# Loading the first half of x first, sharing one bank between the first two products of eight pairs, and moving the second layer's memory keys in a two-layer fp32 network

## The chip, the cores and the metric

The kernel runs on one core of one Trainium2 chip. The metric is device time in microseconds (us) of one execution; with several executions, their median. TensorE (PE in the profile) multiplies into banks of PSUM, VectorE (DVE) and ScalarE (ACT) read those banks and work on SBUF, GpSimd (POOL) works on SBUF, and SyncE (SP) issues the transfers (DMA).

## What is computed

Two layers over 1024 tokens of width 1024, with a memory of 256 rows, all in fp32:

```python
def reference(x, mem, norm_g, final_g, mem_norm_g, ...):
    mem_n = rmsnorm(mem, mem_norm_g)
    h = x
    for i in range(DEPTH):                 # 2
        j = i // 2
        if i % 2 == 0:
            h = even_layer(h, mem_n, ...)
        else:
            h = odd_layer(h, mem_n, ...)
    return rmsnorm(h, final_g)

def even_layer(h, mem_n, g, w_in, pool_w, pool_scale, w_mem_kv, w_out):
    u = rmsnorm(h, g)
    za, rq, rk, rv, xq, gate = split_cols(u @ w_in, EVEN_SPLITS)
    y = concat([pool_mixer(za), retention(rq, rk, rv), mem_attention(xq, mem_n, w_mem_kv)]) * silu(gate)
    return h + y @ w_out

def odd_layer(h, mem_n, ...):
    u = rmsnorm(h, g)
    q, kc, vc, ks, vs, kw, vw, gl, xq, gate = split_cols(u @ w_in, ODD_SPLITS)
    y = concat([nsa_attention(q, kc, vc, ks, vs, kw, vw, gl), mem_attention(xq, mem_n, w_mem_kv)]) * silu(gate)
    return h + y @ w_out
```

`mem_attention` needs keys and values of the memory, `mem_n @ w_mem_kv`, in both layers. `nsa_attention` compresses keys (`kc`, `vc`), selects blocks by them, and attends to the selected blocks (`ks`, `vs`) and to a window (`kw`, `vw`).

## The kernel before

Activations lie transposed: 128 features on the partitions, 512 tokens (half of the 1024, `HT`) in the free dimension, so one half of x is 8 tiles of 128x512. The fp32 products are made of three matmuls each: `split` (L70, L71) cuts a tile into a rounded high part, cast by ScalarE, and the rest, subtracted by VectorE or by GpSimd, and `mm3` (L77 to L79) multiplies high by high, low by high and high by low. In the names, `wh` and `wl` are the parts of a weight tile, `wr` is the raw one, `uh` and `ul` those of the normalised input. A scheduler fixes the order of each engine's instructions from the program's order; tiles come from pools with a fixed number of buffers, and a tile that takes a buffer waits for the last readers of the one before it.

**Start.** `mem_kv("ev")` (L296) loads the memory (`memT`, two transfers), forms its scaled parts `mu`, its sum of squares `macc`, and multiplies by four weight tiles for the keys (256 columns a matmul) and four for the values (512 columns). Only then `make_u` (L436) loads the first half of x (`x`, four buffers), sums the squares into `acc`, and takes the reciprocal root: the sum over partitions is a matmul with ones (L135), the root's power is taken by GpSimd (L142), VectorE multiplies the identity by it (`dg`, L150), a matmul with ones spreads it over all partitions (L155), ScalarE copies it to `rb` (L158). Then x is loaded a second time, VectorE multiplies each tile by gain and `rb` (`uf`), and it is split. The projections (`ps_mm<-uh,wh`) of the first half follow: pooling, retention, memory attention, gates, two output projections (`out_proj`).

**Half boundary.** The loop over `hf` calls `make_u` for the second half after the first half's last output projection.

**Layer change.** `u_half` (L174) normalises the tiles of the new layer's input, `u_sums` (L182) forms differences of them: the second layer's projections are computed in pairs of weight column blocks by a Strassen scheme over both token halves. Its operands are B11, B21, B22 and T1 to T4, each four tiles of 128x512 in two parts. `strassen` (L226) makes 7 products of 12 matmuls (128x512) for a pair. Two of them need only the first half: B11 and B21. `early` (L206) computes these two ahead for six pairs (kc, vc, q0, q2, q4, q6; `ahead`, L792), while VectorE is still busy with the second half's u; for such a pair `strassen` then makes the other 5. The first product goes to bank a, the second to bank c; ScalarE copies the first out with the scale (L213, tile `p`), VectorE adds the second to it (L220, `sc`). `mem_kv("od")` stands behind them and keeps the memory's parts in the buffers of T4, which is split only afterwards (`u_last`).

**Then** the remaining pairs run, with `rel_tables`, `compress`, `select` (the choice of blocks, L955 on, its scores at L992) and the memory heads between them.

**Start of attention.** `kv_prep` (L1110) fetches the keys and values of each of two groups, four tiles of keys (`kraw`) and four of values (`vraw`) a group, through two buffers called uf, splits the keys, and transposes the values on TensorE (L120). Group 0 is prepared before the first head, group 1 behind the first head's scores.

Of the kernel before, what the change touches and what calls it, by code (L numbers as in the profile page):

```python
# [9 lines left out]
F32 = mybir.dt.float32  # L10
# [9 lines left out]
HT = 512  # L20
# [19 lines left out]
def net(tc, a, out, dbg=None):  # L40
# [128 lines left out]
        return {nm: [[uo.tile([128, HT], F32R, name=f"{nm}{k}{s}", tag=f"{nm}{k}{s}") for s in "hl"] for k in range(4)]  # L169
                for nm in names}  # L170

    def u_late(uo):
        return [[uo.tile([128, HT], F32R, name=f"T4{k}{s}", tag=f"T4{k}{s}") for s in "hl"] for k in range(4)]

    def u_half(U, x, gi, f, rr, rb):
        rb = spread(rr, HT, r=rb)
        for k in range(8):
# [4 lines left out]
    def u_sums(U, x):  # L182
        for k in range(4):
            b11, b12, b22 = x[0][k], x[1][k], x[1][k + 4]
            dve.tensor_tensor(b11, b12, b11, OP.subtract)
            dve.tensor_tensor(b12, b22, b12, OP.subtract)
            dve.tensor_tensor(b22, b22, b11, OP.subtract)
            split(*U["T2"][k], b22)
            dve.tensor_tensor(x[0][k + 4], x[0][k + 4], b22, OP.subtract)
        for nm, f in (("T3", 1), ("T1", 0)):  # L190
            for k in range(4):
                split(*U[nm][k], x[f][k])

    def u_last(U, uo, x):
        U["T4"] = u_late(uo)
        for k in range(4):
            split(*U["T4"][k], x[0][k + 4])

    def product(o, w, x, start):
        for k in range(4):  # L200
# [5 lines left out]
    def early(U, sa, sink, hold, out_t, scale=1.0):  # L206


        ra = wraw(sa)
        pa = bank("a")  # L210
        product(pa, whl(ra[:, :HT], pool), U["B11"], True)
        t = hold()
        act.activation(t, pa, AF.Copy, scale=scale)  # L213
        pc = bank("c")
        product(pc, whl(ra[:, HT:], pool), U["B21"], True)
        d = dr.tile([128, HT], F32, name=f"p1d{len(kept)}")
        kept.append(d)
        sp.dma_start(d, t)
        c = out_t()
        dve.scalar_tensor_tensor(c, pc, scale, t, OP.mult, OP.add)  # L220
        sink(0, 0, c, None)
        return d

# [72 lines left out]
    def mem_kv(pre, acc, slots, mrb):  # L296


        u = []
        first = not memst  # L300
        for k in range(8):
            if k % 4 == 0:
                r = wraw(a["memT"][k:k + 4].rearrange("k p m -> p k m"))
            x = r[:, (k % 4) * NMEM:(k % 4 + 1) * NMEM]
            s = slots[k // 2][k % 2]
            uh, ul = s[:, :NMEM], s[:, NMEM:]
            act.activation(uh, x, AF.Copy, scale=gains[:, 3, k:k + 1])
            dve.scalar_tensor_tensor(ul, x, gains[:, 3, k:k + 1], uh.bitcast(F32), OP.mult, OP.subtract)
            if first:
                add_square(acc, x, NMEM, k == 0)  # L310
            u.append((uh, ul))
        kd = [dr.tile([128, NMEM], F32, name=f"{pre}mkd{h}") for h in range(4)]
        vd = [dr.tile([128, HT], F32, name=f"{pre}mvd{m}") for m in range(2)]
        mkv[pre] = kd, vd
        for h in range(4):
            w = wload(a[pre + "_mk"][h])
            o = bank("s")
            gemm(o[:, :NMEM], w, u)
            if first and h == 0:
                sp.dma_start(ident, a["ident"])  # L320
                memst["rr"] = rstd_of(acc, NMEM, "m")
            if h == 0:
                rb = spread(memst["rr"], NMEM, r=mrb)
            t = tmp.tile([128, HT], F32, name="mkx", tag="uf", bufs=2)
            dve.tensor_tensor(t[:, :NMEM], o[:, :NMEM], rb, OP.mult)
            sp.dma_start(kd[h], t[:, :NMEM])
        yield
        o2 = [bank("s"), bank("s")]
        for c in range(4):
            w = wload(a[pre + "_mv"][c])  # L330
            for kk in range(2):
                k = 2 * c + kk
                for m in range(2):
                    mm3(o2[m], u[k][0][:, m * 128:(m + 1) * 128], u[k][1][:, m * 128:(m + 1) * 128],
                        w[kk][0], w[kk][1], k == 0, k == 7)
        for m in range(2):
            t = tmp.tile([128, HT], F32, name="mvx", tag="uf", bufs=2)
            act.activation(t, o2[m], AF.Copy, scale=memst["rr"][:, m:m + 1])
            sp.dma_start(vd[m], t)
        yield  # L340
# [92 lines left out]
    evx = ExitStack()  # L433
    tm2 = evx.enter_context(tc.tile_pool(name="tm2", bufs=1, reuse_waits="tile"))

    def make_u(srcs, n, gi, pool_, tag, rr=None):  # L436
        def load(k):
            x = up.tile([128, n], F32, name="x", tag="x", bufs=4)
            sp.dma_start(x, srcs[k])
# [7 lines left out]
        rb = spread(rr, n, r=tm2.tile([128, n], F32, name="rb", tag="rb"))  # L447
        u = []
        for k in range(8):
            uf = tmp.tile([128, n], F32, name="uf", tag="uf", bufs=2)  # L450
            dve.scalar_tensor_tensor(uf, load(k), gains[:, gi, k:k + 1], rb, OP.mult, OP.mult)
            uh = pool_.tile([128, n], F32R, name="uh", tag=tag, bufs=16)
            ul = pool_.tile([128, n], F32R, name="ul", tag=tag, bufs=16)
            split(uh, ul, uf)
            u.append((uh, ul))
# [65 lines left out]
    def drain(g):  # L521
        for _ in g:
            pass

    with tc.tile_pool(name="mk0", bufs=1, reuse_waits="tile") as mp_:
        macc, mrb = (mp_.tile([128, NMEM], F32, name=nm) for nm in ("macc", "mrb"))
        slots = [[mp_.tile([128, HT], F32R, name=f"mu{k}{x}") for x in "hl"] for k in range(4)]
        drain(mem_kv("ev", macc, slots, mrb))

    rh = []  # L530
    ep = evx.enter_context(tc.tile_pool(name="ep", bufs=1, reuse_waits="tile"))
    if True:
# [9 lines left out]
        R = [None] * 4  # L542

        for hf in range(2):
            u = make_u([a["xT"][k][:, hf * HT:(hf + 1) * HT] for k in range(8)], HT, 0, up, "u")
            if hf == 0:
                hacc = []
                retm = econst("retm", (128, 4, 128))
# [99 lines left out]
            with tc.tile_pool(name="rp", bufs=1, reuse_waits="tile") as rp:  # L648
# [101 lines left out]
                ret_out(0, n0)  # L750
                ret_out(1, n1)
            if hf == 0:
                out_proj(1, EV_ORDER[1], False)


# [17 lines left out]
    kvs = ctx.enter_context(tc.tile_pool(name="kvs", bufs=1, reuse_waits="tile"))  # L773
    ulx = ExitStack()
    uo = ulx.enter_context(tc.tile_pool(name="uo1", bufs=1, reuse_waits="tile"))
    U.update(u_pool(uo, ("T3", "T1", "T2", "B22")))

    qd = dram2("qd", 12)
    zo = {nm: dram2("o" + nm, n)
# [19 lines left out]
    ahead(("kc", 0), ("vc", 0))  # L799
    u_half(U, X, 1, 1, rh[1], wtile("rb"))  # L800
    u_sums(U, X)
    ahead(("q", 0), ("q", 2), ("q", 4), ("q", 6))
    drain(mem_kv("od", None, u_late(uo), wtile("mrb")[:, :NMEM]))
    u_last(U, uo, X)
    xpx.close()

    def mem_heads(p_, pre, xq, gate, dst, bufs=1, pbufs=1):
# [250 lines left out]
    proj_pair("vc", 0)  # L1058
    proj_pair("q", 0)
    rel_tables()  # L1060
    proj_pair("q", 2)
    compress()
    proj_pair("q", 4)
# [43 lines left out]
        dve.memset(t[:, 0:256], 0.0)  # L1107
        tabs.append(t)

    def kv_prep(g):  # L1110
        for f in range(2):
            c = slice(f * HT, (f + 1) * HT)
            for br in ("s", "w"):
                k = fetch(tmp, zo["k" + br][g][f], "uf", 2, "kraw")
                split(KT[br, g][0][:, c], KT[br, g][1][:, c], k)
                v = fetch(tmp, zo["v" + br][g][f], "uf", 2, "vraw")
                b = bank("t", (128, 4, 128))
                for n in range(4):
                    transpose(b[:, n], v[:, n * 128:(n + 1) * 128])
                split(VN[br, g][0][:, 4 * f:4 * f + 4], VN[br, g][1][:, 4 * f:4 * f + 4], b)  # L1120

    with ExitStack() as oc:
# [147 lines left out]
                proj.pop(0)  # L1270

        proj_step()
        kv_prep(0)
        res = []
        for _ in scores(*units[0], res):
            proj_step()
        kv_prep(1)
        for n, (hf, h) in enumerate(units):
            now, res = res, []
            sg = scores(*units[n + 1], res) if n + 1 < len(units) else iter(())  # L1280
# [149 lines left out]
```

## Time and profile before

| | us |
|---|---|
| median of 3 runs | 2050.36 (2049.96 to 2052.46) |
| the profiled execution | 2047.62 |
| its span in the trace | 2045.8 |
| mean granted clock of TensorE | 0.976 |
| TensorE busy | 1944.2 (95%) |
| VectorE busy | 1276.0 (62%) |
| ScalarE busy | 943.0 (46%) |
| GpSimd busy | 598.7 (29%) |

The span runs from the first to the last instruction of the core; the execution's own time lies 1.8 us above it. Busy time of TensorE includes the overlap of successive matmuls, so a share of 95% doesn't say how fast it works. A row of the waits names the engine and instruction that waited, and what ended the wait. A row of the timeline has start and duration, and in brackets how long the engine had been idle before and what released it.

### The profile page before, as it was taken

The page shows a single profiled execution, that of the slowest core. Times are in us where ns is not written, and L with a number is a line of the kernel's source. Part 1 is how long each engine was busy: PE and PEld are TensorE (multiplying, and loading weights), DVE is VectorE, ACT ScalarE, POOL GpSimd, SP SyncE. Part 2 cuts the span into 40 slices and gives each one's busy share as a digit, 9 for nine tenths or more (in the row PEclk, how much of TensorE's full clock was granted, in tenths as well). Part 3 has the DMA queues.
Part 4 walks back from the last instruction along what each step waited for, and adds up shares of the span by engine and source line. Part 5 has one row for each costly group of instructions (what it writes and reads, how often), then busy time and mean ns, then how long its engine had stood idle before and what let it go on. Part 6 is the DMA issues. An engine that isn't in the chain of part 4 may idle for free.

```text
span 2045.8 us, 28686 instructions
## 1 busy us (share of the span) xinstructions
PE 1944.2 (95%) x9814; PEld 1618.4 (79%) x9814; DVE 1276.0 (62%) x2741; ACT 943.0 (46%) x1867; POOL 598.7 (29%) x615
## 2 busy tenths in 40 slices
PE   5799999999999999799999999998899999999996
PEld 4688888878888877678878788886788888888885
DVE  4667455566645564745439855765666677877675
ACT  4445322334432243431222344544656676767674
POOL 0111110010311002245426643333343444333422
PEclk9899999989999999899999999998899999999998
DMA  6423234442222444476535433337454532151312
GB/s 208 154 82 129 89 107 134 146 141 83 92 93 84 143 152 153 153 209 204 183 114 185 149 106 125 134 108 249 141 177 148 165 99 73 46 172 47 114 37 93
DMA packets 128246, 267.07 MB, mean 131 GB/s; under 512 B 15543, under 2 KB 32707, under 8 KB 128067
## 3 DMA queue, kind: packets, MB, share of 16 engines
q1 hardware_dynamic: 128100, 265.24, 40.0%
q8 instruction: 77, 1.26, 0.3%
q14 instruction: 69, 0.57, 0.1%
HBM read 206.97 MB, written 60.57 MB: 131 GB/s over the span
## 4 chain that ended last, share of the span: by engine, by line
PE 48%; DVE 3%; DMA 2%; issue 1%; ACT 1%; POOL 0%; SPq 0%; DVEq 0%; POOLq 0%; ACTq 0%
PE ps_t L120 5%; PE ps_a L77 3%; PE ps_a L78 3%; PE ps_a L79 3%; PE ps_s L77 3%; PE ps_mm L77 3%; PE ps_mm L79 3%; PE ps_s L78 3%; PE ps_s L79 3%; PE ps_mm L78 3%; PE ps_o L84 2%; PE ps_o L83 2%; PE ps_o L82 2%; PE ps_b L77 2%; PE ps_b L78 2%; PE ps_b L79 2%
## 5 line engine op out<-in xcount | busy, mean ns | idle before, releaser
L70 ACT CAST wh<-wr 128x512 fp32r<-128x512 f32 (+1 forms) x395 | 242.1, 618 | 475.0 <-PE ps_mm L78 312.1
L71 DVE TENSOR_TENSOR wl<-wr,wh 128x512 fp32r<-128x512 f32 (+1 forms) x281 | 213.8, 766 | 173.6 <-ACT wh L70 167.7
L77 PE MATMUL ps_mm<-uh,wh 128*128 128x512 f32 x640 | 253.6, 398 | 2.7 <-ACT uh L70 2.7
L71 POOL TENSOR_TENSOR wl<-wr,wh 128x512 fp32r<-128x512 f32 x114 | 158.6, 1393 | 325.4 <-ACT wh L70 292.2
L79 PE MATMUL ps_mm<-uh,wl 128*128 128x512 f32 x640 | 253.3, 396 | 0.0
L78 PE MATMUL ps_mm<-ul,wh 128*128 128x512 f32 x640 | 253.2, 396 | 0.0
L77 PE MATMUL ps_mm<-yh,wh 128*128 128x512 f32 x512 | 205.9, 408 | 7.0 <-ACT yh L70 4.1
L79 PE MATMUL ps_mm<-yh,wl 128*128 128x512 f32 x512 | 206.6, 405 | 1.8 <-DVE wl L71 1.5
L78 PE MATMUL ps_mm<-yl,wh 128*128 128x512 f32 x512 | 206.9, 404 | 0.0
L71 DVE TENSOR_TENSOR apl<-ps_t,aph 128x512 fp32r<-128x512 f32 x204 | 136.1, 671 | 44.9 <-ACT aph L70 34.2
L70 ACT CAST aph<-ps_t 128x512 fp32r<-128x512 f32 x204 | 114.9, 568 | 87.2 <-PE ps_o L83 45.3
L77 PEld LDWEIGHTS ps_mm<-uh,wh 128*128 128x128 f32 x640 | 121.3, 190 | 28.3 <-ACT uh L70 4.4
L1205 POOL TENSOR_TENSOR Pw<-Pw,arc 128x640 f32<-128x640 f32 (+2 forms) x96 | 96.2, 1002 | 161.2 <-DVE arc L1201 98.2
L78 PEld LDWEIGHTS ps_mm<-ul,wh 128*128 128x128 f32 x640 | 121.4, 190 | 24.6 <-DVE ul L71 0.4
L79 PEld LDWEIGHTS ps_mm<-uh,wl 128*128 128x128 f32 x640 | 121.3, 190 | 24.7
L77 PEld LDWEIGHTS ps_mm<-yh,wh 128*128 128x128 f32 x512 | 96.9, 191 | 29.2 <-ACT yh L70 5.0
L70 ACT CAST wh<-ws 128x512 fp32r<-128x512 f32 x88 | 54.1, 618 | 141.4 <-PE ps_a L78 67.5
L79 PEld LDWEIGHTS ps_mm<-yh,wl 128*128 128x128 f32 x512 | 97.5, 191 | 23.3 <-DVE wl L71 2.6
L78 PEld LDWEIGHTS ps_mm<-yl,wh 128*128 128x128 f32 x512 | 97.5, 190 | 20.4 <-DVE yl L71 0.7
L71 DVE TENSOR_TENSOR wl<-ws,wh 128x512 fp32r<-128x512 f32 x88 | 68.2, 776 | 59.1 <-ACT wh L70 55.7
L1197 ACT ACTIVATE Ps<-Ps,anm 128x512 f32<-128x512 f32 (+3 forms) x96 | 74.6, 777 | 28.3 <-DVE anm L1194 27.9
L1207 ACT ACTIVATE Ps<-Ps,arc 128x512 f32<-128x512 f32 (+3 forms) x96 | 74.7, 778 | 20.7 <-DVE arc L1201 19.5
(893 smaller groups left out, 4820.1 us busy)
## 6 DMA issues: line engine op xcount, KB each, us to landing
wr<-in_ev_gate SPq DMA_DIRECT2D x32, 512.0 KB, 3.5
wr<-in_ev_out SPq DMA_DIRECT2D x32, 512.0 KB, 3.5
wr<-in_od_out SPq DMA_DIRECT2D x64, 256.0 KB, 3.2
oa<-oho SPq DMA_DIRECT2D x52, 256.0 KB, 2.1
oxr<-oa SPq DMA_DIRECT2D x52, 256.0 KB, 2.8
x<-in_xT SPq DMA_DIRECT2D x32, 256.0 KB, 3.6
wr<-in_od_q SPq DMA_DIRECT2D x16, 512.0 KB, 3.7
w<-in_cmp_w SPq DMA_DIRECT2D x16, 512.0 KB, 4.7
```

The source lines that it names most:

```text
L70: act.copy(hi, src)
L71: (eng or dve).tensor_tensor(lo, src, hi.bitcast(F32), OP.subtract)
L77: pe.matmul(o, wh, xh, start=start, stop=False, skip_group_check=skip)
L78: pe.matmul(o, wh, xl, start=False, stop=False, skip_group_check=skip)
L79: pe.matmul(o, wl, xh, start=False, stop=stop, skip_group_check=skip)
L82: pe.matmul(o, wh, xh, start=start, stop=False)
L83: pe.matmul(o, wl, xh, start=False, stop=False)
L84: pe.matmul(o, wh, xl, start=False, stop=stop)
L120: pe.transpose(o, x, ident[:k, :k])
L1197: act.activation(pt, pt, AF.Exp, bias=nm[:, bi:bi + 1], accum_out=su[:, bi:bi + 1])
L1205: pool.tensor_tensor(pt, pt, rc[:, bi:bi + 1].to_broadcast(list(pt.shape)), OP.mult)
L1207: act.activation(pt, pt, AF.Copy, scale=rc[:, bi:bi + 1])
```

## The change

1. **Start.** The identity and the first half's 8 tiles (`xs`) are loaded before the memory and stay in SBUF; the squares go into `xacc`. `make_u` of the first half is called before the memory's products are drained, and multiplies in place in `xs`: these tiles are not loaded again. The second half's `make_u` is called ahead of the first half's last output projection.
2. **Early pairs.** Both products of a pair add up in one bank, taken in turn from a, a, b, c. ScalarE copies it out after the first product (L205) and again after the second (L211). The low parts of both weights are made by VectorE. Two more pairs, xq0 and xq2, are computed ahead: eight.
3. **Memory of the second layer.** `mem_kv("od")` is called behind `rel_tables`, with buffers of its own; T4 is an operand like the others.
4. **Staging.** `kv_prep` takes a function: group 0 is fetched through the six buffers `Pw`, group 1 through the eight `Ps` (two of each of four), all of the attention's pool.

```diff
     def early(...):
         ra = wraw(sa)
-        pa = bank("a")
-        product(pa, whl(ra[:, :HT], pool), U["B11"], True)
+        b = bank("aabc"[len(kept) % 4])
+        product(b, whl(ra[:, :HT]), U["B11"], True)
         t = hold()
-        act.activation(t, pa, AF.Copy, scale=scale)
-        pc = bank("c")
-        product(pc, whl(ra[:, HT:], pool), U["B21"], True)
+        act.activation(t, b, AF.Copy, scale=scale)
         d = dr.tile([128, HT], F32, name=f"p1d{len(kept)}")
         kept.append(d)
         sp.dma_start(d, t)
+        product(b, whl(ra[:, HT:]), U["B21"], False)
         c = out_t()
-        dve.scalar_tensor_tensor(c, pc, scale, t, OP.mult, OP.add)
+        act.activation(c, b, AF.Copy, scale=scale)
         sink(0, 0, c, None)
...
-    def make_u(srcs, n, gi, pool_, tag, rr=None):
+    def make_u(srcs, n, gi, pool_, tag, rr=None, xs=None):
...
-            uf = tmp.tile([128, n], F32, name="uf", tag="uf", bufs=2)
-            dve.scalar_tensor_tensor(uf, load(k), gains[:, gi, k:k + 1], rb, OP.mult, OP.mult)
+            uf = xs[k] if xs else tmp.tile([128, n], F32, name="uf", tag="uf", bufs=2)
+            dve.scalar_tensor_tensor(uf, xs[k] if xs else load(k), gains[:, gi, k:k + 1], rb, OP.mult, OP.mult)
...
+    sp.dma_start(ident, a["ident"])
     with tc.tile_pool(name="mk0", bufs=1, reuse_waits="tile") as mp_:
+        xs = [mp_.tile([128, HT], F32, name=f"xs{k}") for k in range(8)]
+        acc = mp_.tile([128, HT], F32, name="xacc")
+        for k in range(8):
+            sp.dma_start(xs[k], a["xT"][k][:, :HT])
+            add_square(acc, xs[k], HT, k == 0)
...
-        drain(mem_kv("ev", macc, slots, mrb))
+        mem = mem_kv("ev", macc, slots, mrb)
+        u = make_u(None, HT, 0, up, "u", rstd_of(acc, HT), xs)
+        drain(mem)
...
         for hf in range(2):
-            u = make_u([a["xT"][k][:, hf * HT:(hf + 1) * HT] for k in range(8)], HT, 0, up, "u")
...
             if hf == 0:
+                u = make_u([a["xT"][k][:, HT:] for k in range(8)], HT, 0, up, "u")
                 out_proj(1, EV_ORDER[1], False)
...
-    ahead(("q", 0), ("q", 2), ("q", 4), ("q", 6))
-    drain(mem_kv("od", None, u_late(uo), wtile("mrb")[:, :NMEM]))
-    u_last(U, uo, X)
+    ahead(("q", 0), ("q", 2), ("q", 4), ("q", 6), ("xq", 0), ("xq", 2))
...
     rel_tables()
+    with tc.tile_pool(name="mk1", bufs=1, reuse_waits="tile") as mp_:
+        mrb = mp_.tile([128, NMEM], F32, name="mrb1")
+        slots = [[mp_.tile([128, HT], F32R, name=f"mv{k}{x}") for x in "hl"] for k in range(4)]
+        drain(mem_kv("od", None, slots, mrb))
     proj_pair("q", 2)
...
-                k = fetch(tmp, zo["k" + br][g][f], "uf", 2, "kraw")
+                k = stage(zo["k" + br][g][f], "kraw")
...
-        kv_prep(0)
+        kv_prep(0, lambda src, nm: fetch(at, src, "Pw", PW, nm))
...
-        kv_prep(1)
+        turn = iter(range(8))
+        kv_prep(1, lambda src, nm: fetch(at, src, f"Ps{next(turn) % 4}", PB, nm))
```

How instructions stand now: SyncE at the start of the program, before (`x` are the first half's tiles, `ev_mk` the memory's key weights):

```order
L112 DMA c_gains<-in_gains 128x32
L89 DMA wr<-in_memT 128x4x256 x2
L320 DMA c_ident<-in_ident 128x128
L439 DMA x<-in_xT 128x512 x4
L89 DMA wr<-in_ev_mk 128x1024
L439 DMA x<-in_xT 128x512
L89 DMA wr<-in_ev_mk 128x1024 x3
L89 DMA wr<-in_ev_mv 128x1024
```

and after (`xs` are the first half's tiles, `x` now the second half's):

```order
L515 DMA c_ident<-in_ident 128x128
L520 DMA xs_129<-in_xT 128x512
L520 DMA xs_130<-in_xT 128x512
L520 DMA xs_131<-in_xT 128x512
L520 DMA xs_132<-in_xT 128x512
L520 DMA xs_133<-in_xT 128x512
L520 DMA xs_134<-in_xT 128x512
L520 DMA xs_135<-in_xT 128x512
L520 DMA xs_136<-in_xT 128x512
L89 DMA wr<-in_memT 128x4x256 x2
L429 DMA x<-in_xT 128x512 x5
L89 DMA wr<-in_ev_mk 128x1024 x4
```

The memory moved behind eight tiles of x, and its first weights behind five more, of the second half.

VectorE at the start, before, from the memory's sum of squares on (`wl` are low parts of weights, `mkx` finished keys):

```order
L129 TENSOR_TENSOR macc<-macc,sq 128x256 x5
L71 TENSOR_TENSOR wl<-wr,wh 128x512 x2
L140 TENSOR_SCALAR rs<-ps_t 128x2
L150 TENSOR_SCALAR dg<-c_ident,rrkm 128x128 x2
L71 TENSOR_TENSOR wl<-wr,wh 128x512 x4
L325 TENSOR_TENSOR mkx<-ps_s,mrb 128x256
```

and after:

```order
L441 SCALAR_TENSOR_TENSOR xs_129<-xs_129,c_gains,rb 128x512
L441 SCALAR_TENSOR_TENSOR xs_130<-xs_130,c_gains,rb 128x512
L441 SCALAR_TENSOR_TENSOR xs_131<-xs_131,c_gains,rb 128x512
L441 SCALAR_TENSOR_TENSOR xs_132<-xs_132,c_gains,rb 128x512
L441 SCALAR_TENSOR_TENSOR xs_133<-xs_133,c_gains,rb 128x512
L441 SCALAR_TENSOR_TENSOR xs_134<-xs_134,c_gains,rb 128x512
L441 SCALAR_TENSOR_TENSOR xs_135<-xs_135,c_gains,rb 128x512
L441 SCALAR_TENSOR_TENSOR xs_136<-xs_136,c_gains,rb 128x512
L129 TENSOR_TENSOR macc<-macc,sq 128x256
L71 TENSOR_TENSOR ul<-xs_129,uh 128x512
L71 TENSOR_TENSOR ul<-xs_130,uh 128x512
L71 TENSOR_TENSOR wl<-wr,wh 128x512 x2
```

The first weights' low parts now stand behind the eight products of x by `rb` and two low parts of u.

TensorE at the layer change, before, where the first product of kc (B11, bank a) ends and the second (B21, bank c) begins:

```order
L78 MATMUL ps_a_7065<-B113l_6554,wh_7066 128x512
L79 MATMUL ps_a_7065<-B113h_6553,wl_7067 128x512
L77 MATMUL ps_c_7084<-B210h_6555,wh_7085 128x512
L78 MATMUL ps_c_7084<-B210l_6556,wh_7085 128x512
L79 MATMUL ps_c_7084<-B210h_6555,wl_7086 128x512
```

and after, the fifth pair, q4, at the same step:

```order
L78 MATMUL ps_a_7290<-B113l_6530,wh_7291 128x512
L79 MATMUL ps_a_7290<-B113h_6529,wl_7292 128x512
L77 MATMUL ps_a_7290<-B210h_6531,wh_7311 128x512
L78 MATMUL ps_a_7290<-B210l_6532,wh_7311 128x512
L79 MATMUL ps_a_7290<-B210h_6531,wl_7312 128x512
```

Here both products stand one behind the other in one bank. In the pairs before it seven products in all stand between (the order begins with the first products of kc and vc, the spread of the second half's root at L155, ten matmuls of q0's first product, then the second products of kc and vc); in q6 two matmuls do.

At the half boundary the sum of squares (L135, `acc`) stood behind the last matmul of the first half and the spread (L155) directly behind it; now the sum stands behind the first matmul of the last output projection, and 31 matmuls of that projection lie between it and the spread.

More of the change, by code (lines that the diff above doesn't have):

```diff
@@ L170, in u_pool @@
                 for nm in names}
-    def u_late(uo):
-        return [[uo.tile([128, HT], F32R, name=f"T4{k}{s}", tag=f"T4{k}{s}") for s in "hl"] for k in range(4)]
     def u_half(U, x, gi, f, rr, rb):
@@ L189, in u_sums @@
             dve.tensor_tensor(x[0][k + 4], x[0][k + 4], b22, OP.subtract)
-        for nm, f in (("T3", 1), ("T1", 0)):
+        for nm, f, k0 in (("T3", 1, 0), ("T1", 0, 0), ("T4", 0, 4)):
             for k in range(4):
[L192 to L197, printed above, removed]
+                split(*U[nm][k], x[f][k + k0])
     def product(o, w, x, start):
@@ L319, in mem_kv @@
             if first and h == 0:
-                sp.dma_start(ident, a["ident"])
                 memst["rr"] = rstd_of(acc, NMEM, "m")
@@ L775, in net @@
     uo = ulx.enter_context(tc.tile_pool(name="uo1", bufs=1, reuse_waits="tile"))
-    U.update(u_pool(uo, ("T3", "T1", "T2", "B22")))
+    U.update(u_pool(uo, ("T3", "T1", "T2", "B22", "T4")))
     qd = dram2("qd", 12)
@@ L1108, in net, with kv_prep @@
         tabs.append(t)
-    def kv_prep(g):
+    def kv_prep(g, stage):
         for f in range(2):
@@ L1113, in kv_prep @@
             for br in ("s", "w"):
-                k = fetch(tmp, zo["k" + br][g][f], "uf", 2, "kraw")
+                k = stage(zo["k" + br][g][f], "kraw")
                 split(KT[br, g][0][:, c], KT[br, g][1][:, c], k)
-                v = fetch(tmp, zo["v" + br][g][f], "uf", 2, "vraw")
+                v = stage(zo["v" + br][g][f], "vraw")
                 b = bank("t", (128, 4, 128))
```

## The prediction

> **What bounds the kernel now.** First the page: of its 40 slices of 51 us, here TensorE and its granted clock.
>
> ```profile
> PE   5799999999999999799999999998899999999996
> PEclk9899999989999999899999999998899999999998
> ```
>
> TensorE is full except in the first two slices, near slice 16 (the layer change), slices 27 and 28 (the start of attention) and the last. Work taken off other engines is worth nothing elsewhere; what counts is TensorE's waits and the slow clock behind them. So next the waits of TensorE, in order of cost (us in total, times, longest):
>
> ```profile
> PE ps_t L135 <- DVE acc L129: 15.7, 1, 15.7
> PE ps_t L135 <- DVE macc L129: 13.8, 1, 13.8
> PE ps_t L120 <- DMA vraw<-ovs: 7.4, 2, 6.3
> PE ps_t L155 <- DVE dg L150: 6.8, 3, 2.8
> PE ps_t L120 <- DMA vraw<-ovw: 6.2, 2, 3.2
> PE ps_c L77 <- DVE sc L220: 6.0, 1, 6.0
> PE ps_s L79 <- DVE wl L71: 2.9, 1, 2.9
> ```
>
> The first two are the start; the dg wait of 2.8 us is the half boundary; ps_c and ps_s are the layer change; vraw is the start of attention. Then each of these stages by windows (length, busy time of TensorE, weight loads, VectorE, ScalarE, GpSimd, granted clock, DMA share, GB/s):
>
> ```profile
> 0.00:66.40 66.40, 31.39 (x160) 25.73 (x161) 31.91 (x68) 29.09 (x57) 2.12 (x10) 0.85 0.62 204
> 66.40:71.00 4.60, 4.60 (x11) 3.62 (x12) 4.58 (x7) 1.85 (x3) 0.00 (x0) 0.53 0.64 203
> 427.40:439.40 12.00, 8.64 (x23) 6.39 (x23) 8.74 (x18) 4.00 (x7) 2.43 (x2) 0.57 0.53 173
> 806.40:883.90 77.50, 63.21 (x295) 51.96 (x294) 51.92 (x87) 33.10 (x62) 19.92 (x11) 0.91 0.48 154
> 883.90:890.00 6.10, 6.10 (x14) 4.28 (x14) 5.29 (x6) 2.29 (x4) 3.78 (x3) 0.50 0.43 138
> 1049.80:1136.30 86.50, 84.60 (x458) 72.46 (x456) 68.00 (x118) 26.65 (x47) 57.26 (x57) 0.98 0.51 168
> 1397.00:1441.00 44.00, 34.77 (x158) 28.30 (x158) 25.90 (x69) 25.96 (x58) 20.69 (x24) 0.88 0.96 317
> 1441.00:1453.30 12.30, 6.89 (x31) 5.67 (x32) 4.81 (x9) 4.94 (x9) 3.00 (x3) 0.58 0.53 166
> ```
>
> The clock is a second cost: behind each stage with waits lies a stretch near 0.5. The timeline shows what that does to one 128x512 matmul (start, duration):
>
> ```profile
> 67.42 0.63 PE L78 MATMUL ps_mm<-ul,wh 128*128 128x512 f32 x1
> 67.85 0.63 PE L79 MATMUL ps_mm<-uh,wl 128*128 128x512 f32 x1
> 71.74 0.39 PE L78 MATMUL ps_mm<-ul,wh 128*128 128x512 f32 x1
> 71.97 0.39 PE L79 MATMUL ps_mm<-uh,wl 128*128 128x512 f32 x1
> ```
>
> They follow each other in 0.43 us at half clock and in 0.23 at full, so half of the busy time at half clock is lost. Every TensorE price below goes by starts (0.23), not by durations.
>
> **The change part by part.** *Start.* The timeline:
>
> ```profile
> 1.18 0.97 SPq L89 DMA_DIRECT2D wr<-in_memT  x2
> 10.91 0.33 SPq L89 DMA_DIRECT2D wr<-in_ev_mk  x1
> 14.39 1.14 ACT L70 CAST wh<-wr 128x512 fp32r<-128x512 f32 x2 [1.24 <-DMA wr<-in_ev_mk]
> 15.06 0.58 PE L77 MATMUL ps_s<-mu0h,wh 128*128 128x256 f32 x1 [0.23 <-ACT wh L70]
> 57.29 0.69 DVE L129 TENSOR_TENSOR acc<-acc,sq 128x512 f32<-128x512 f32 x1 [0.63 <-ACT sq L128]
> 58.12 1.84 PE L135 MATMUL ps_t<-ones,acc 128*128 128x1 f32 x8 [15.66 <-DVE acc L129]
> 64.33 0.58 ACT L158 COPY rb<-ps_t 128x512 f32<-128x512 f32 x1 [5.13 <-PE ps_t L155]
> 64.95 1.41 DVE L451 SCALAR_TENSOR_TENSOR uf<-x,c_gains,rb 128x512 f32<-128x512 f32 x2 [2.78 <-ACT rb L158]
> 66.40 1.22 PE L77 MATMUL ps_mm<-uh,wh 128*128 128x512 f32 x2 [2.11 <-ACT uh L70]
> ```
>
> Before: memory products 15.1 to 42.5 (58.12 less 15.66), 27.4 us; then nothing until the sum of squares; the projections run from 66.4, the first 4.6 us at 0.53, so in effect from 68.6. After: eight tiles of 256 KB are 2.1 MB, at the 317 GB/s of the attention window 6.6 us, landed about 9; eight adds of squares at 0.69 behind them end about 12. From the sum to rb took 58.1 to 64.9, 6.8 us: rb about 19. Eight uf at 0.7 end about 25. The first weights of the memory are now issued behind all that SyncE has queued and wait for a buffer that the memory's squares free late, about 18.5; landing took 3.5, so 22. Their low halves stand on VectorE behind the eight uf and two ul: the products start about 27. Then 27.4 us of products, with waits of 1 to 5 us (second weights; dg of the memory now behind two wl): they end at 55 to 59.5, and the projections follow at once at full clock. I take 59.5, since VectorE also has eight ul to make among them: gain 68.6 - 59.5 = **9**. Bounds: 14 with no wait and a start 1 us earlier, 2 where the products start at 34.
>
> *Half boundary.*
>
> ```profile
> 430.20 2.05 PE L155 MATMUL ps_t<-dg,ones 128*128 128x512 f32 x2 [2.75 <-DVE dg L150]
> 434.36 1.22 PE L77 MATMUL ps_mm<-uh,wh 128*128 128x512 f32 x2 [0.61 <-ACT uh L70]
> ```
>
> The second half's loads and squares now begin during the first half, and some 30 matmuls (7 us) stand between the sum's row and the spread's, as long as the 6.8 us chain. Gone: 2.75 + 0.61, and half of what ran at half clock, the 2.05 of the spread and the 5.0 of projections from 434.4 to 439.4: 3.5. I leave 0.4 for the cover being tight: **6.5**, bounds 4 and 7.
>
> The Trainium skill, "TensorE: Matmul & The Clock Gate", Part 1 (the clock gate), has the clock fall after about 3.4 us of idle. The row speaks against it: a wait of 2.75 us and a clock of 0.57. By the page the slow stretch isn't this wait's, and this part would give 2.75 + 0.61 less the 0.4, 3.0.
>
> *Layer change.* Timeline rows, then groups of 806 to 884:
>
> ```profile
> 816.42 5.50 DVE L178 SCALAR_TENSOR_TENSOR x<-x,c_gains,rb 128x512 f32<-128x512 f32 x8 [3.44 <-ACT rb L158]
> 836.19 0.59 ACT L213 ACTIVATE p<-ps_a 128x512 f32<-128x512 f32 x1
> 839.51 0.80 PE L77 MATMUL ps_c<-B210h,wh 128*128 128x512 f32 x1 [5.98 <-DVE sc L220]
> ```
>
> ```profile
> L71 DVE TENSOR_TENSOR wl<-wr,wh 128x512 fp32r<-128x512 f32 x16 | 10.7, 687 | 6.9 <-ACT wh L70 6.8
> L220 DVE SCALAR_TENSOR_TENSOR sc<-ps_c,p 128x512 f32<-128x512 f32 x6 | 4.1, 685 | 8.6 <-PE ps_c L79 8.6
> L71 POOL TENSOR_TENSOR wl<-wr,wh 128x512 fp32r<-128x512 f32 x7 | 15.3, 2200 | 14.0 <-ACT wh L70 14.0
> ```
>
> TensorE's work in the window: six pairs of 24 matmuls and 48 of the memory's at 0.23 (44.2), 96 of 256 columns at half (11.0, an estimate from the 0.23), sums and spreads 1.8: 57 of 77.5. Lost: 20.5, and half of the 6.1 behind it, 3.05: 23.5. After: eight pairs, 192 x 0.23 = 44.2, against the u chain on VectorE. Its sc are gone (4.1), the memory's steps too; 16 wl come, 12 of them inside the chain (12 x 0.69 = 8.2). The spread stands after two products, so rb comes about 813.6 instead of 816.4, and by its rows at 0.6 to 0.7 the chain ends about 848, while the pairs end about 853 and cover it. Where both products of a pair share a bank, the second waits for the copy. In TensorE's order other products lie between, but at two of the eight only two matmuls or none: 0.8 each. The second bound is the 5.98 above, which came from an eviction queued behind u steps; ScalarE's queue has casts of the u chain ahead of its copies too, so it is kept for a rival. With 1.9 of waits here, and 1.6 for the memory's products in their new place among pairs (theirs waited 2.9 for wl here): **20**, bounds 14 and 23.
>
> The Trainium skill, "PSUM — Partial Sum Buffer", summary of rules, has a matmul write another bank while one is read. If nothing lay between, all eight pairs would pay the 0.59 copy and its hand-over, 6 to 8 us in all, and the sum would be 35.
>
> *Select.* In 1049.8 to 1136.3 VectorE is busy 68.0 of 86.5, making the selection beside pairs on TensorE. Two pairs of xq give up two products each, 48 x 0.23 = 11 us, and most of that lay here: the stage shrinks towards 75.5 with VectorE's 68.0, a chain of dependent steps, still to do. Of these 11 I take back **-2**, bounds 0 and -4.
>
> *Attention.*
>
> ```profile
> 1441.62 0.63 PE L120 MATMUL ps_t<-c_ident,vraw 128*128 128x128 f32 x4 [3.01 <-DMA vraw<-ovw]
> 1449.31 1.09 PE L120 MATMUL ps_t<-c_ident,vraw 128*128 128x128 f32 x4 [3.18 <-DMA vraw<-ovw]
> ```
>
> The second group's tiles come one by one through two buffers. In 1441 to 1453.3 TensorE idles 5.4, with 2.4 of the 3.01 ahead of the window 7.8, and loses 2.9 of 6.89 to the clock: 10.7. With eight buffers I leave 1.7, and 0.5 for loads that crowd the first group (the DMA share there is 0.96): **8.5**, bounds 4 and 11. The 6.3 for the first vraw stays: its load hangs on the last projections.
>
> Sum: 9 + 6.5 + 20 - 2 + 8.5 = 42. The profiled execution took 2047.62 (span 2045.8), so 2005.6; it lies 2.7 under the median of 2050.36, so **2008**.
>
> **The rivals.** *The shared bank stalls the pairs* (slower): each second product waits until ScalarE, behind a cast that waits for VectorE, has copied the first. At 5.98 a pair this costs 48, the gain is gone and the time is 2056; it decides from 5.2 a pair. For it: the same wait at 839.51, and the copies among casts. Against: seven products between in most places. 0.04.
>
> *The start gains nothing.* VectorE works on uf and ul first, the memory's weights come late, products end at 66 to 68: 2017. For it: the weights stand behind 17 transfers. 0.13.
>
> *The moved work stalls where it goes.* The memory's weights pass through two buffers among pairs that need their own, and select waits on VectorE: its ten transfers of 3.5 us take 35 us against 23 of products, 12 back, 2020. For it: VectorE's 68.0 in select and the DMA share of 0.51 there. Against: the pairs around it have work to put between. 0.13.
>
> *The clock's loss stays.* If the slow stretches don't hang on the removed waits, 2.3 + 3.5 + 3.05 + 2.9 don't come back: 2020. The rows speak against it, since each stretch follows a wait. It is what the rule of the Trainium skill's clock page, above, would make of waits under 3.4 us. 0.07.
>
> *All covers hold*: start and attention reach their upper bounds, 7.5 more: 2000. 0.08.
>
> **How the numbers follow.** Forecast 0.55; its own range is 2000 to 2016, as the five parts won't all lie at the same bound. With the rivals at 2017 to 2020 and a stall or two beside them, 1994 to 2026 leaves out the slower rival and thin tails. This kernel's times spread by 0.1%, so 0.2% (4 us) is what can be told from no change: faster 0.94, same 0.02, slower 0.04.
>
> **What would show it.** Right: the first memory product at 26 to 28, no wait of several us between it and the second half; no dg wait and a clock of 1 at the half boundary; pairs without gaps for 46 to 48 us behind the last sum, a Strassen product directly behind; no vraw wait above 2 for the second group. Wrong: a wait of ps_a, ps_b or ps_c on ScalarE's p1 of over 1 us in several pairs; waits on wr of the memory's weights among the pairs; slow-clock stretches where no wait stands ahead.

## The result, and the profile after

The changed kernel takes 2018.80 us (median of 4 runs, 2017.64 to 2021.65) against 2050.85 (median of 4 as well): a ratio of 0.9845, 95% interval [0.9828, 0.9862], 32 us. The profiled execution took 2021.65, the longest of the four, with a span of 2019.8 where before had 2045.8; a second profile of the same program, taken later beside experiments, has a span of 2013.3. Both are used below, since what differs between them can't be the change; whether both ran on the same chip isn't known.

The page of the first, slices counted from 0: the first slice has 4 for TensorE, the second is full, and the dips of before at slices 16 and 28 are gone. One at slice 27 is left, and single ones at 17 and 22 are new: there lie the memory's new place and select.

```profile
PE   4999999999999999989999899998999999999996
PEclk9999999999999999999999999998999999999998
```

The starts of the same instructions in three traces (timeline, us) show where the time went:

| | before | after | after, second profile |
|---|---|---|---|
| first projection of the first half | 66.4 | 63.1 | 62.5 |
| last sum of squares before the layer change | 805.5 | 791.6 | 791.0 |
| first Strassen product with T2 | 883.9 | 844.7 | 842.4 |
| last product before the attention | 1394.5 | 1378.0 | 1372.2 |
| end | 2045.8 | 2019.8 | 2013.3 |

By the second profile: 14.5 us are gained up to the layer change (forecast: 15.5), 7.8 between there and the attention (forecast: 18), 10.2 from there on (forecast: 8.5). The sum is 32.5, where 42 was forecast.

TensorE's waits now (us in total, times, longest):

```profile
PE ps_t L135 <- DVE xacc L129: 13.7, 1, 13.7
PE ps_mm L77 <- ACT yh L70: 10.4, 2, 9.0
PE ps_t L155 <- DVE dg L150: 8.1, 3, 5.0
PE ps_b L77 <- ACT mv3l L298: 4.2, 1, 4.2
PE ps_s L77 <- ACT wh L70: 3.8, 1, 3.8
PE ps_s L79 <- DVE wl L71: 3.7, 1, 3.7
PE ps_b L77 <- DVE sc L245: 3.6, 1, 3.6
PE ps_a L77 <- ACT wh L70: 2.2, 1, 2.2
PE ps_a L77 <- ACT p L205: 1.0, 2, 0.7
```

The two waits for sums of squares that cost 15.7 and 13.8 have become one of 13.7, the wait of 6.0 for VectorE's sum at the layer change is gone, and so are those for vraw; of the last, the part at the first values now stands at yh (9.0, start of attention). New are the first wh and wl (ps_s, the start) and mv3l (the memory's new place); sc at L245 (select, L254 before) grew from 1.3 to 3.6. p at L205 is the copy between the two products of one bank: 1.0 in all.

Windows of the start and of the half boundary (length, TensorE, weight loads, VectorE, ScalarE, GpSimd, clock, DMA share, GB/s), then the start's waits and VectorE's queue there:

```profile
23.00:64.00 41.00, 30.30 (x154) 26.30 (x155) 24.50 (x47) 15.89 (x32) 1.08 (x1) 0.92 0.44 140
416.00:430.00 14.00, 14.00 (x66) 11.52 (x64) 6.05 (x9) 4.86 (x8) 0.60 (x1) 1.00 0.51 170
```

```profile
24.10 0.58 PE L77 MATMUL ps_s<-mu0h,wh 128*128 128x256 f32 x1 [3.75 <-ACT wh L70]
28.59 0.58 PE L79 MATMUL ps_s<-mu0h,wl 128*128 128x256 f32 x1 [3.69 <-DVE wl L71]
42.29 1.22 PE L155 MATMUL ps_t<-dg,ones 128*128 128x256 f32 x2 [4.98 <-DVE dg L150]
44.44 0.58 PE L77 MATMUL ps_s<-mu0h,wh 128*128 128x256 f32 x1 [0.92 <-DVE mkx L315]
```

```profile
21.00 5.39 DVE L441 SCALAR_TENSOR_TENSOR xs<-xs,c_gains,rb 128x512 f32<-128x512 f32 x8 [0.63 <-ACT rb L158]
26.64 1.29 DVE L71 TENSOR_TENSOR ul<-xs,uh 128x512 fp32r<-128x512 f32 x2
27.84 1.29 DVE L71 TENSOR_TENSOR wl<-wr,wh 128x512 fp32r<-128x512 f32 x2
39.20 1.29 DVE L71 TENSOR_TENSOR wl<-wr,wh 128x512 fp32r<-128x512 f32 x2 [4.24 <-ACT wh L70]
41.76 0.48 DVE L150 TENSOR_SCALAR dg<-c_ident,rrkm 128x128 f32<-128x128 f32 x2
```

The half boundary is as forecast: no idle, clock 1.00. At the start two memory products run at 24.1, but then TensorE stands 3.7 us until VectorE, through with the eight uf and two ul, has made the first wl (27.84): the first product with a low part, for which the forecast had 27, comes at 28.6. Later it waits 5.0 for dg. The memory's squares were long summed (the last ended at 35.0, the sum over partitions ran at 36.8); ahead of dg on VectorE stand four wl, and the first two wait 4.24 us for their casts (39.20), as ScalarE itself waits 4.4 us for that weight tile. Its transfer comes late: SyncE needs from 19.9 to 35.0 to issue the four tiles of key weights.

The memory's new place among the Strassen pairs, with ScalarE and VectorE ahead of the stall:

```profile
888.12 0.51 ACT L298 ACTIVATE mv2h<-wr,c_gains 128x256 fp32r<-128x256 f32 x1 [5.56 <-DMA wr<-in_memT]
888.66 0.48 DVE L299 SCALAR_TENSOR_TENSOR mv2h<-wr,c_gains,mv2h 128x256 fp32r<-128x256 f32 x1 [3.77 <-ACT mv2h L298]
889.06 0.68 DVE L245 TENSOR_TENSOR sc<-ps_b,u 128x512 f32<-128x512 f32 x1
889.89 0.47 PE L77 MATMUL ps_b<-T10h,wh 128*128 128x512 f32 x1 [4.17 <-ACT mv3l L298]
```

ScalarE stood 5.6 us at the memory's second transfer. VectorE's step of the memory (mv2h) waits for ScalarE, and behind it stands the sum `sc<-ps_b,u` of the pair before, which reads bank b; the next product into bank b starts 0.15 us after that sum ends (889.74), 4.2 us late. The row names mv3l because it ended last, at 889.82, but this product reads nothing of the memory; in a run below (memory transfers ahead) the same wait is put down to the sum, again 0.15 us after its end. In the second profile the two waits around the memory measure 3.6 (mv3l) and 3.6 (q2's pair behind it, whose weights were issued only at 910.2, behind the memory's eight weight tiles), with a slow-clock stretch of 3.4 us after each.

### The profile page after: what moved, and what is told of

Same layout as the page of the kernel before. It is cut to its first block, busy times and chain, and to the rows that moved or that the text cites. A ratio compares the mean times of both kernels' runs of the same rounds, so it can differ in the third digit from the quotient of the medians.

```text
span 2019.8 us, 28659 instructions
## 1 busy us (share of the span) xinstructions
PE 1937.2 (96%) x9814; PEld 1611.9 (80%) x9814; DVE 1276.8 (63%) x2753; ACT 942.8 (47%) x1869; POOL 570.2 (28%) x601
## 4 chain that ended last, share of the span: by engine, by line
PE 85%; DVE 7%; DMA 3%; ACT 2%; issue 2%; POOL 1%; SPq 0%; DVEq 0%; POOLq 0%; ACTq 0%
PE ps_mm L79 13%; PE ps_mm L77 13%; PE ps_mm L78 13%; PE ps_t L120 6%; PE ps_s L77 4%; PE ps_s L78 3%; PE ps_s L79 3%; PE ps_a L77 3%; PE ps_a L78 3%; PE ps_a L79 3%; PE ps_o L84 2%; PE ps_o L82 2%; PE ps_o L83 2%; PE ps_b L77 2%; PE ps_b L79 2%; PE ps_b L78 2%
## 5 line engine op out<-in xcount | busy, mean ns | idle before, releaser
L71 DVE TENSOR_TENSOR wl<-wr,wh 128x512 fp32r<-128x512 f32 (+2 forms) x295 | 219.4, 749 | 178.8 <-ACT wh L70 170.3
L71 POOL TENSOR_TENSOR wl<-wr,wh 128x512 fp32r<-128x512 f32 x100 | 134.1, 1342 | 225.9 <-ACT wh L70 150.5
L71 DVE TENSOR_TENSOR wl<-ws,wh 128x512 fp32r<-128x512 f32 x88 | 77.8, 890 | 52.2 <-ACT wh L70 48.7
L1207 ACT ACTIVATE Ps<-Ps,arc 128x512 f32<-128x512 f32 (+3 forms) x96 | 74.6, 778 | 19.4 <-DVE arc L1201 18.5
```

The source lines that it names most:

```text
L71: (eng or dve).tensor_tensor(lo, src, hi.bitcast(F32), OP.subtract)
L1207: act.activation(pt, pt, AF.Copy, scale=rc[:, bi:bi + 1])
```

## The experiments

Theory: each step works by the mechanism forecast, and what is missing of 42 us is in two places, the start (9 us of waits where up to 5 were forecast) and the memory's new place with select behind it. Rivals: a step gains nothing by itself (the shared bank stalls, say), or what one step gains is lost further down. Every kernel is compared with the kernel before on its own chip. The ratios of the changed kernel are 0.9845 (the result above) and 0.9843 (run again beside the last three variants). Beside the four variants from memory first to memory back it was not run, so these compare by ratio.

**Start alone** (on the kernel before).

```diff
+    sp.dma_start(ident, a["ident"])
...
-        drain(mem_kv("ev", macc, slots, mrb))
+        mem = mem_kv("ev", macc, slots, mrb)
+        u = make_u(None, HT, 0, up, "u", rstd_of(acc, HT), xs)
+        drain(mem)
```

> The kernel before with part 1's first step alone: the first half's tiles loaded first and kept, its root formed ahead of the memory's products. My theory (the step works, but the memory's products start late and wait twice): projections start at about 63 at full clock, 5.5 us gained, 2045. Rival (the step gains the 9 forecast and the rest was lost elsewhere): 2042. Rival (the memory now ends so late that nothing is gained): 2050.

Measured: 2042.79 against 2048.62, ratio 0.9975 [0.9965, 0.9984]; first projection at 62.4. The time looks like the rival's 2042, but the kernel before is faster here than in the expectation; the gain, 5 to 6 us (at most 7 by the interval, not 9), and the start of the projections are the theory's.

**Half boundary alone.**

```diff
-            u = make_u([a["xT"][k][:, hf * HT:(hf + 1) * HT] ...)
             if hf == 0:
+                u = make_u([a["xT"][k][:, :HT] ...)
...
+                u = make_u([a["xT"][k][:, HT:] ...)
                 out_proj(1, EV_ORDER[1], False)
```

> The kernel before with the second half's normalisation alone called ahead of the first half's last output projection. Theory: no dg wait and no slow clock at the boundary, 7.7 us gained, 2043. Rival by the rule that only idle of over 3.4 us slows the clock: the two gaps of 2.75 and 0.61 go, the slow stretch stays, 3.4 gained, 2047.5.

Measured: 2047.79, ratio 0.9998 [0.9989, 1.0006]: nothing. Yet the gap at the boundary and its slow clock are gone, and the last sum before the layer change comes at 800.0 instead of 805.5. So the gain was there and was lost between the layer change and the attention (594.2 us there against 589.0) and behind it. Neither of the two expectations names this. The lead is still 5.1 us at the first product with T2 (878.8 against 883.9) and 0.5 at twelve matmuls of the compression (939.7 against 940.2). Here is SyncE's queue ahead of the compression, in this run and then in the kernel before:

```profile
905.95 2.37 SPq L919 DMA_DIRECT2D kcf<-okc  x3
911.91 0.33 SPq L89 DMA_DIRECT2D wr<-in_od_q  x1
912.30 0.42 SPq L919 DMA_DIRECT2D kcf<-okc  x1
914.67 0.98 SPq L931 DMA_DIRECT2D w<-in_cmp_w  x2
```

```profile
908.88 5.07 SPq L918 DMA_DIRECT2D kcf<-okc  x4
915.89 0.91 SPq L930 DMA_DIRECT2D w<-in_cmp_w  x2
```

The scheduler now put a weight load (wr) ahead of the last kcf; it waits for its buffer until 911.9, and the compression's weights, which SyncE issues in order behind it, come 1.2 us earlier while TensorE comes 5 earlier. It waits for them:

```profile
PE ps_s L939 <- DMA w<-in_cmp_w: 3.4, 2, 2.8
```

**Pairs alone** (`early` of the change in the kernel before; six pairs, memory in its old place).

```diff
-        pa = bank("a")
+        b = bank("aabc"[len(kept) % 4])
...
-        pc = bank("c")
-        product(pc, whl(ra[:, HT:], pool), U["B21"], True)
+        product(b, whl(ra[:, HT:]), U["B21"], False)
...
-        dve.scalar_tensor_tensor(c, pc, scale, t, OP.mult, OP.add)
+        act.activation(c, b, AF.Copy, scale=scale)
```

> The kernel before with the first two products of its six pairs in one bank, both copies by ScalarE, low parts of weights by VectorE; the memory's products stay at the layer change. Theory (the pairs run as forecast, the loss is the memory's new place): the wait of 6.0 for the sum on VectorE goes with the slow clock behind it (3.4), the memory's own waits stay, about 8 gained, 2043. Rival (the copies between the two products stall TensorE): no wait less in sum, 2049 to 2056.

Measured: 2043.72, ratio 0.9983 [0.9973, 0.9993]: 3.5 us gained by the ratio and 4.9 by the medians, of 8 expected. The profile is of one of the longest executions (2047.60). TensorE's waits from 806 to 930:

```profile
PE ps_a L77 <- ACT wh L70: 4.7, 2, 4.0
PE ps_s L77 <- ACT wh L70: 3.2, 2, 2.7
PE ps_s L937 <- DMA w<-in_cmp_w: 2.6, 1, 2.6
PE ps_a L77 <- ACT p L213: 0.9, 2, 0.7
```

The wait of 6.0 is gone, the copies between two products (p) cost 0.9 in all: the rival of the stalling bank falls. The same late weights of the compression as in the run above, 2.6, may take part of the expected 8.

**Staging alone** (on the kernel before).

```diff
-        kv_prep(0)
+        kv_prep(0, lambda src, nm: fetch(at, src, "Pw", PW, nm))
...
-        kv_prep(1)
+        kv_prep(1, lambda src, nm: fetch(at, src, f"Ps{next(turn) % 4}", PB, nm))
```

> The kernel before with the staging of keys and values alone changed (six buffers for the first group, eight for the second). Theory: the second group's waits for values go with the slow clock there, 9 gained, 2042; the wait at the first values stays at 6 or moves to the memory part's y. Rival (loads crowd each other): 3 gained, 2048.

Measured: 2038.33, ratio 0.9956 [0.9944, 0.9968], 9 to 10 us (6.6 to 11.5 by the interval). No vraw is left among the waits of 1394 to 1460; the one for the first values went to the memory part's y, as expected:

```profile
PE ps_mm L77 <- ACT yh L70: 9.6, 1, 9.6
```

**Memory first at the start** (on the changed kernel).

```diff
+        raw = [wraw(a["memT"][k:k + 4]...) for k in (0, 4)]
...
+        rr0 = rstd_of(acc, HT)
         mem = mem_kv("ev", macc, slots, mrb, raw)
-        u = make_u(None, HT, 0, up, "u", rstd_of(acc, HT), xs)
+        next(mem)
+        u = make_u(None, HT, 0, up, "u", rr0, xs)
         drain(mem)
```

The memory's keys stand ahead of uf and ul, its values behind them.

> The changed kernel with another start: the memory's two transfers first, then the eight tiles of x; the squares of x, then the memory's keys, then uf and ul of x, then the values. Theory (the start lost 9.6 us in waits because the memory's weights came late and stood behind x on VectorE and in SyncE's queue): products from about 20, projections from 48 to 50 instead of 63, ratio to before 0.9845 less 0.0065, about 2005 where the changed kernel has 2018. Rival (the products' waits have another cause, or what is gained is lost later as in the run with the half boundary alone): 2012 to 2018.

Measured: 2012.07, ratio 0.9821 [0.9806, 0.9836]. The waits of the start, up to 66 us:

```profile
PE ps_t L135 <- DVE xacc L129: 17.1, 1, 17.1
PE ps_s L78 <- DVE wl L71: 4.0, 2, 3.7
```

A single matmul of the projections runs at 48.7, between the last value products; then TensorE waits 3.7 for a wl, and the projections proper begin at 54.8, at half clock until 56.1, where 48 to 50 was expected. The last sum before the layer change comes at 784.4 instead of 791.6, so the 7 us gained at the start are kept that far. The time is 2012 where 2005 was expected, at the edge of the rival's range; TensorE now waits 17.1 for x at the very start. The wait for dg is gone, so that it came from the order of the queues holds; the size did not.

**Memory transfers ahead** (on the changed kernel).

```diff
+        raw = [mp_.tile([128, 1024], F32, name=f"mr{k}") for k in range(2)]
+        for k in range(2):
+            sp.dma_start(raw[k]..., a["memT"][4 * k:4 * k + 4]...)
...
-        drain(mem_kv("od", None, slots, mrb))
+        drain(mem_kv("od", None, slots, mrb, raw))
```

> The changed kernel, but the memory's two transfers of the second layer go into buffers of their own and are issued ahead of its products. Theory (ScalarE's queue stands still for 5.6 us until the second of them has landed, and the casts of the pair behind it make TensorE wait 4.2 with a slow window behind): 4 to 6 us gained, 2012 to 2014. Rival (the pair's own weights or its VectorE steps come as late): 2018.

Measured: 2016.70, ratio 0.9841 [0.9826, 0.9856], no difference from the changed kernel's 0.9845. The time is the rival's, but the transfers were not early: SyncE issued them at 857.7, and ScalarE waits for them as long as before.

```profile
865.70 0.51 ACT L298 ACTIVATE mv0h<-mr,c_gains 128x256 fp32r<-128x256 f32 x1 [6.82 <-DMA mr<-in_memT]
870.62 0.68 DVE L245 TENSOR_TENSOR sc<-ps_b,u 128x512 f32<-128x512 f32 x1
871.45 0.77 PE L77 MATMUL ps_b<-T10h,wh 128*128 128x512 f32 x1 [3.26 <-DVE sc L245]
```

ScalarE stands 6.8 us, only earlier, and the pair's sum stands on VectorE behind the memory's eight steps (866.2 to 870.7): a wait of 3.3 in place of 4.2. So this run doesn't tell the transfer from the steps behind it.

**Six pairs** (on the changed kernel).

```diff
-    ahead(("q", 0), ("q", 2), ("q", 4), ("q", 6), ("xq", 0), ("xq", 2))
+    ahead(("q", 0), ("q", 2), ("q", 4), ("q", 6))
```

> The changed kernel with the six pairs of before computed ahead; xq0 and xq2 are made whole again beside the selection. Theory (select lacked TensorE work beside a full VectorE, 2.1 and 3.6 of waits with two slow windows): 5 us come back in select, but 11 us of cover are missing at the layer change, where the u chain ends about 848 and the pairs at 842: 2018 to 2021. Rival (the two more pairs cost nothing in select and pay at the layer change): 2022 to 2026.

Measured: 2023.59, ratio 0.9875 [0.9859, 0.9892], 6 us slower than the changed kernel. From 800 to 930:

```profile
PE ps_a L77 <- ACT wh L70: 10.0, 3, 4.1
PE ps_b L77 <- ACT mv3l L298: 2.0, 1, 2.0
```

The rival holds: the cover is missing at the layer change (6.3 of the 10.0 stand before 870), and in select only the smaller wait (1.5 to 2.1) goes. The one for a sum stays at 3.4 without the two early xq pairs, so it isn't their doing.

**Memory back at the layer change** (on the changed kernel).

```diff
     ahead(("q", 0), ("q", 2), ("q", 4), ("q", 6), ("xq", 0), ("xq", 2))
     xpx.close()
+    with tc.tile_pool(name="mk1", bufs=1, reuse_waits="tile") as mp_:
...
+        drain(mem_kv("od", None, slots, mrb))
...
     rel_tables()
-    with tc.tile_pool(name="mk1", bufs=1, reuse_waits="tile") as mp_:
...
```

> The changed kernel with the second layer's memory products back at the layer change, right behind the eight pairs, in buffers of their own. Theory (the new place costs 4.2 and 2.2 with two slow windows, 10 in all): no wait among the Strassen pairs; the memory's transfers are issued under the early pairs, so 4 to 8 gained, 2010 to 2014. Rival (it is a matter of the memory's two-buffer weight stream wherever it stands): its waits return at the new place, 2016 to 2020.

Measured: 2022.20, ratio 0.9871 [0.9857, 0.9886], 5 us slower. From 800 to 930:

```profile
PE ps_a L77 <- ACT wh L70: 7.2, 2, 5.0
PE ps_s L77 <- ACT wh L70: 2.5, 2, 2.3
```

The theory falls here, and the time lies even above the rival's 2016 to 2020: waits of 9.7 where the new place has 6.4 to 7.1. The longest, 5.0, stands at the first product with T2, directly behind the memory's products (873.2): its weights were issued at 863.4, behind the last of the memory's. So in both places the pair behind the memory waits for weights issued behind the memory's. That the two weight buffers are the cause was not tested; no run gives the stream more buffers.

**Without the half boundary's step** and **without the start's** (each undone in the changed kernel).

```diff
-                u = make_u([a["xT"][k][:, HT:] for k in range(8)], HT, 0, up, "u")
                 out_proj(1, EV_ORDER[1], False)
...
         for hf in range(2):
+            if hf == 1:
+                u = make_u([a["xT"][k][:, HT:] for k in range(8)], HT, 0, up, "u")
```

```diff
-        u = make_u(None, HT, 0, up, "u", rstd_of(acc, HT), xs)
...
+        drain(mem_kv("ev", macc, slots, mrb))
...
             if hf == 0:
+                u = make_u([a["xT"][k][:, :HT] for k in range(8)], HT, 0, up, "u")
```

> The changed kernel with the second half's normalisation back at the half boundary. Theory (its 6 to 8 us are real at the boundary; in the run with this step alone they were lost further down, where the compression's weights came late, and in the changed kernel there is no such wait): ratio to before 0.9845 plus 0.003, 2024 where the changed kernel has 2018. Rival (what is gained there is lost again further down in any order): 2018 to 2019.

> The changed kernel with the start of before: memory first, x behind it, x loaded twice. Theory (the step's 5 us are kept to the end): 2023. Rival (given back): 2018 to 2019.

Measured beside the changed kernel itself, whose expectation was

> The changed kernel itself beside the other three, as their measure on this chip: 2017 to 2019; its stages within 1.5 us of the first profile, except where the slow clock's windows fall otherwise (3.4 us of slow clock cost 1.7).

2024.63 (ratio 0.9882 [0.9863, 0.9902]) and 2022.57 (0.9873 [0.9854, 0.9891]), the changed kernel 2017.01 (0.9843 [0.9827, 0.9859]). The half boundary's step is worth 7.6 us in it, though it was worth 0.8 alone; the start's 5.6. With the first undone, the two waits are back, and the clock from 415 to 440 is 0.86, 3.5 us lost, which makes 7.6 in all:

```profile
PE ps_t L155 <- DVE dg L150: 2.8, 1, 2.8
PE ps_mm L77 <- ACT uh L70: 1.3, 1, 1.3
```

In the changed kernel the memory's products stand ahead of the compression, whose weights are no longer late (no w among its waits): what was lost there in the run with the half boundary alone seems to be kept.

**Both variants** (memory first at the start, memory transfers ahead).

> The changed kernel with the memory-first start and the second layer's memory transfers ahead in their own buffers, the two variants that were not slower. Theory (independent places): 2010, 8 below the changed kernel. Rival (the second gives nothing, as one wait only made room for another): 2012 as with the start alone.

Measured: 2009.07, ratio 0.9806 [0.9787, 0.9824], against 2017.01 on the same chip: it beats both kernels by 8 us and more. Whether the second variant adds to the first's 0.9821 the intervals don't tell. The profile does show what the second alone couldn't: here SyncE issued the memory's transfers at 849.8, ScalarE waits 2.1 for them, and the wait of bank b for the sum is 0.5, where the run with memory first alone has 2.3. So in this profile an earlier transfer goes with a shorter stall.

## Why the forecast was right, and where it was off

The way and the range held; the time came 11 us above the likeliest value and above the forecast's own 2000 to 2016; it lies in the range because that was drawn to take in the rivals. The rival "the moved work stalls where it goes" (2020, chance 0.13) comes nearest in time and in mechanism, but part of the loss is the start's. Two of the signs of being wrong appeared: waits for the memory's transfers among the pairs, and a slow stretch with no wait ahead (at 843, in one profile of two).

- *Half boundary* (6.5 forecast): 7.6 in the changed kernel. The gap of 2.75 and the slow stretch go together, so the row and not the 3.4 us rule of the Trainium skill ("TensorE: Matmul & The Clock Gate", Part 1) gave the right price; the page's rule would have given 3.0.
- *Attention* (8.5): 9 to 10 alone.
- *Shared bank* (1.9 of waits, and a slower rival at 0.04): p waits 1.0 in the changed kernel, 0.9 in the run with the pairs alone. The rule of "PSUM — Partial Sum Buffer" in the Trainium skill, by which all eight pairs would pay if nothing lay between, prices another order: here other products lie between in six of eight. No run shows the copies with nothing between in all pairs.
- *Start* (9): 5.6. The mis-sized term is "waits of 1 to 5 us": 3.7, 5.0 and 0.9 were measured, 9.6, and a slow stretch of 6.8 us (41 to 48) fell on and behind the 5.0; some 4.2 of it were work, so about 2 lost. The sign "no wait of several us" there did not hold. I had dg behind wl, rightly, but left out that these wl would themselves wait for late weights.
- *Layer change* (20) and *select* (-2): 7.8 together by the second profile. The failed term is "1.6 for the memory's products in their new place": 7.1 of waits and two slow stretches of 3.4 us, each costing half of it, 10.5. I priced them by the wl wait of the old place; left out were the memory's steps on ScalarE and VectorE, which wait for the transfer with a pair's sum behind them, and the weights of the pair behind, which SyncE issues after the memory's. From the last sum to the first T2 product the second profile has 51.4, where 46 to 48 were forecast for the pairs. A slow stretch follows the last sum of squares at 792 as well (1.7), where before had none behind the same wait. In select the two waits are 1.5 and 3.6 in the second profile, where before had 1.3 and 1.9; the run with six pairs shows that the larger one isn't due to the early xq pairs. It is bank b again, waiting for a pair's sum on VectorE, here behind steps of select with no idle time between (first profile):

```profile
1135.03 1.75 DVE L994 TENSOR_TENSOR sc<-sc,cmx 128x512 f32<-128x512 f32 x1
1136.70 0.68 DVE L245 TENSOR_TENSOR sc<-ps_b,u 128x512 f32<-128x512 f32 x1
1137.43 0.80 PE L77 MATMUL ps_b<-T10h,wh 128*128 128x512 f32 x1 [3.57 <-DVE sc L245]
```

- Sums that don't close: two waits of 0.8 are 1.6 and not 1.9, and paying at all eight pairs would leave 36 to 38 and not 35, as the 1.9 was already taken off. Neither moves the forecast by more than 2 us.
- What is only argued: that the order of SyncE's queue is what ate the half boundary's gain in the run with it alone. One profile of that run shows the late weights; their 3.4 us of waiting are most of the 4.6 lost in that stretch, and no run mends the queue to see the gain come back.

## What to carry to other kernels

A step moved between others is priced with all its instructions on every in-order queue it enters: here a transfer awaited by ScalarE and short steps on VectorE, with a pair's sum behind them, made TensorE stand, and not the matmuls. A wait row names what ended last; where the named instruction has nothing to do with the waiting one, look for what frees its bank. A gain measured alone can be anything from nothing to its full size, as a scheduler orders the queues anew; undo each step in the finished kernel as well. Before believing a stage of one profile, take a second one of the same program and see what differs by itself.

## What the runs showed of the hardware

The slow clock differed in stretches of 3.4 us between two executions of one program. Windows of the changed kernel, first profile and second, around four places with the same waits (0.6 to 3.6 us) or none:

```profile
738.00:750.00 12.00, 9.40 (x27) 6.88 (x28) 11.28 (x18) 8.67 (x16) 0.00 (x0) 0.72 0.97 359
790.00:800.00 10.00, 8.35 (x27) 7.01 (x28) 3.56 (x11) 1.75 (x3) 1.01 (x1) 0.66 0.12 47
843.00:853.00 10.00, 10.00 (x41) 7.14 (x39) 3.21 (x6) 1.90 (x5) 5.63 (x4) 0.83 0.50 147
1133.00:1145.00 12.00, 8.43 (x25) 6.43 (x24) 9.44 (x13) 3.75 (x7) 7.62 (x7) 0.72 0.38 131
```

```profile
738.00:750.00 12.00, 8.87 (x28) 6.17 (x28) 11.32 (x19) 8.51 (x15) 0.00 (x0) 0.86 0.93 335
790.00:800.00 10.00, 9.00 (x35) 7.13 (x36) 3.24 (x11) 2.32 (x5) 1.01 (x1) 0.83 0.22 78
841.00:851.00 10.00, 10.00 (x52) 7.62 (x51) 4.19 (x5) 2.16 (x5) 4.70 (x5) 1.00 0.53 164
1129.00:1141.00 12.00, 8.43 (x30) 6.55 (x30) 9.44 (x13) 3.42 (x7) 7.85 (x7) 0.86 0.39 131
```

In each the clock differs by 0.14 over 12 us or 0.17 over 10, 1.7 us lost or 3.4 at half clock: 13.6 in all, which can cost half, 6.8 us, and the spans differ by 6.5 (2019.8 against 2013.3). On one chip, four executions of the changed kernel spread by 3.3 us (2015.06 to 2018.35). At 843 the profile counts TensorE busy throughout, but small products of `rel_tables` (33 rows, 12 columns) run there from 843.2 to 846; whether they count as idle for the clock no run here shows. That the clock goes by free-running windows is what the Trainium skill says in the section named above ("TensorE: Matmul & The Clock Gate", Part 1); that it needs 3.4 us of idle first is not what the rows with waits show.

The clock column can't be trusted at the very start. In the first profile the 256-column matmuls follow each other in 0.21 us from 29.0 to 33.4 and in 0.12 from 34.3 on, yet the clock there reads 1.00 throughout. The kernel before does the same (0.21 from 16.2 to 19.4), so this changes no comparison.
